# Four layer-norm affines of a two-block transformer step, moved from the passages between phases into the phase that follows

## The chip, the cores and the metric

One core of one Trainium2 chip runs the whole program. The metric is the device time of one execution in microseconds (us), taken over several runs; lower is better. Five engines work side by side, each through its own queue of instructions in a fixed order: PE (matrix multiply into PSUM), DVE (vector), ACT (activation), POOL (GpSimd) and SP, which issues most of the loads.

## The reference

One sequence of 512 tokens, 1024 features, all in float32. Two blocks stand one behind the other, and the program runs them as six phases: `mix` (hybrid mixer), `moe` (16 experts), `mla` (latent attention), `mlp0`, `s5` (a state-space mixer with a gated output) and `mlp1`. Every phase ends in the same step:

```python
x = layer_norm(ALPHA * x + gate * f(h), g, b)     # g, b: 1024 features
h = normalised(x) * (1 + scale) + shift           # what the next phase works on
```

The next phase needs two things of this: `h`, at once, as the input of its matrix products; and the new `x` itself, `normalised * g + b`, only when its own result is added onto it. For `mlp0` and `mlp1` the added row is `b + gate * b2`, b2 being the bias of the phase's second matrix.

## The kernel before

**Tiles.** X is one SBUF tile of [128, 4, 1024]: four token tiles of 128 tokens each. `h` is kept transposed (features on partitions) in two parts, `hh` and `hl`, whose sum is the float32 value, so that each product is three matmuls (`mm3`, lines 118 to 120). A part pair is made by `split_to` (lines 101 and 102): ACT writes the high part, DVE the low part as source minus high part.

**Rings.** Weights are loaded by SP into a ring of five buffers of 4 KB a partition (`wr`), split into rings of three (`wh`, `wl`), and multiplied. The fillers, generators that work out the modulation of later phases (`gemv`, lines 223 to 232), load through the same `wr` ring and add up on ACT, DVE (L228) and POOL (L232). The row tiles of a layer norm (`row_tile`) are taken from the `wr` ring too: g and b, each 512 KB as one row of 4 KB spread over all partitions, occupy two of its five buffers until they are used up.

**A passage.** A phase closes with `out_last` (or `combine` in `moe`): it loads its last weights, calls `begin_next`, and then runs the four token tiles through a pipeline. `begin_next` finishes the next phase's modulation, opens its `hh` and `hl`, and loads the two rows by `ln_rows` (with `b + gate * b2` for an mlp: two half rows of b2, two POOL multiplies at L371 and two POOL adds at L372). Each token tile is added up by DVE, gets its statistics (L296, L289, and the small column operations of `rsqrt`, L262 to L274, and L292), is normalised by ACT (L303), transposed by PE (L323), scaled and shifted out of PSUM by ACT (L333) and DVE (L331), and split into hh and hl. Then `affine_X` multiplies X[t] by g (L349) and adds b (L350), both on POOL, 128x1024 each. So a passage has eight POOL instructions of that size, and four passages have them: moe to mla, mla to mlp0, mlp0 to s5, s5 to mlp1.

**The places that the change names.** In `mla` the heads are walked in blocks of 128 queries, u = 0, 1, 2, ...; `probs` ends in the DVE scaling L468, kept as `self.scaled`. At u = 0 the weights of head 1 are loaded (`straight`, L529 and L530), at u = 4 those of head 2; at u = 5 the first three filler loads (L223) are given out, held by line 553 until the scaling of u = 4 is done; at u = 6 `rotated` loads the rotary weights of heads 2 and 3 (L514). In `mlp` the first three hidden features f = 0, 1, 2 are multiplied together, half of the tokens after the other (`mlp_first`), and each feature from f = 3 on loads its own 512 KB (L107). Their ReLU is L691, their square L692. In `s5` the gated output has eight features f, each with its own load of 512 KB and a tanh (L2159); after each of them one filler step follows.

**Order.** The tile framework puts each engine's instructions in order ahead of time, by program order and readiness. `after` makes an instruction wait for the end of another one; `hold` does so for what `self.behind` names (in the passage to `mla`, the last indirect gather onto X).

Of the kernel before, what the change touches and what calls it, by code (L numbers as in the profile page):

```python
# [15 lines left out]
D = 1024  # L16
T = 512
NT = 4
# [19 lines left out]
class Kern:  # L38
    def __init__(self, tc, io, ctx):
        self.tc, self.nc, self.io = tc, tc.nc, io  # L40
        nc = self.nc

        def pool(name, bufs, **kw):
            return ctx.enter_context(tc.tile_pool(name=name, bufs=bufs, **kw))

        self.cp = pool("const", 1)
        self.wrp = pool("wr", 5)
        self.whp = pool("wh", 3)
        self.wlp = pool("wl", 3)
        self.xp = pool("xres", 1)  # L50
        self.htp = pool("hT", 1)
        self.tmp = pool("tmp", 6)
        self.gap = pool("ga", 2)
        self.sm = pool("sm", 8)
        self.psA = pool("psA", 4, space=PSUM)
        self.psB = pool("psB", 4, space=PSUM)
        self.fillers = []
        self.behind = self.later = None
        self.consts()

    # ---------------------------------------------------------------- helpers
# [42 lines left out]
    def wload(self, src, kt, n):  # L104
        """src: [kt*128, n] view (or [128, kt, n]); gives the tile [128, kt, n] in two exact parts."""
# [10 lines left out]
    def mm3(self, out, lh, ll, rh, rl, st, sp):  # L116
# [3 lines left out]
        mm(out, ll, rh, start=False, stop=sp)  # L120
# [4 lines left out]
    def hold(self, load):  # L125
        """The load begins after what behind names, if anything."""
        self.after(load, self.behind)

    def after(self, inst, first):
        """inst begins when first, if anything, is done: what follows on first is urgent."""  # L130
# [4 lines left out]
    # ---------------------------------------------------------------- constants  # L135
    def consts(self):
# [11 lines left out]
        # mask[q, k] = 0 where k <= q, NEG elsewhere  # L148
# [6 lines left out]
    def vcols(self, name, parts):  # L155
        """Rows of 128 (features in order) put as columns: returns {key: [128, n] AP}."""
# [14 lines left out]
    # ---------------------------------------------------------------- modulation  # L171
# [15 lines left out]
    def gemv_cols(self, cond, w, n0, bcol, add, dst, p):  # L187
        """dst [128, 8] := part [n0, n0+1024) of cond @ w + b + add, feature-major; on both vector engines, and p
        [128, 8] in PSUM."""
# [23 lines left out]
    def gemv(self, ends, cond, w, b, n0, kind, dst, scale=1.0, bias=0.0):  # L213
        """Part [n0, n0+1024) of cond @ w + b. kind 'col': dst [128, 8] gets it feature-major;
        kind 'row': dst, a row of 1024 in DRAM, gets scale * it + bias. The sums over partitions of a half are put
        into ends and done some steps later, when what they need is there."""
# [40 lines left out]
    # ---------------------------------------------------------------- layer norm  # L257
    def rsqrt(self, out, v, n, eps):
        """out = (v + eps)^-0.5 for [128, n] columns: a guess from the exponent, three Newton steps."""
# [3 lines left out]
        # the guess is negative, and every step changes the sign  # L263
# [12 lines left out]
    def pipeline(self, gens, latest=True):  # L276
        """Generators of stages, each a stage behind the one before it; the latest or the earliest has the way."""
# [7 lines left out]
    def stats(self, st, eps):  # L285
        """From the bn_stats st of both halves: 1 / deviation and -mean / deviation."""
# [11 lines left out]
    def ln_tile(self, t, st, alpha, after):  # L298
        """Stages. X[t] normalised, st its bn_stats, then what follows on token tile t.
        (The norm of alpha times what X[t] holds, whose eps is alpha**2 times the one here.)"""  # L300
# [5 lines left out]
    def early(self, t, h, y, gate):  # L306
        """X[t] += gate * y for one half, y in PSUM (gate: what the reference multiplies by, over alpha)."""
# [6 lines left out]
    def to_hT(self, t, src, G, B, perm=False):  # L314
        """Stages. Token tile t (token-major src [128, 1024]) -> its columns of hT, times G plus B, in two parts.
        perm: token 256 h + 8 k + j stands at column 256 h + 32 j + k."""
# [29 lines left out]
    def affine_X(self, t, g, cb):  # L346
        """X[t] := X[t] * g + cb, off the main line."""
        nc = self.nc
        nc.gpsimd.tensor_mul(self.X[:, t], self.X[:, t], g)  # L349
        nc.gpsimd.tensor_add(self.X[:, t], self.X[:, t], cb)  # L350
# [8 lines left out]
    def ln_rows(self, g, b, gate=None, b2=None):  # L359
        """Row tiles g and b + gate * b2 on every partition."""  # L360
# [3 lines left out]
        self.bcast_row(gt, g, D)  # L364
        self.bcast_row(bt, b, D)
        if b2 is not None:
            for h in range(2):
                c = slice(512 * h, 512 * h + 512)
                tt = self.t()
                self.bcast_row(tt, b2[c], 512)  # L370
# [4 lines left out]
    def mod_gen(self, cond, w, b, g_col, b_col, key, out, alpha, dram):  # L375
        """shift, scale -> G, B columns; (1 + gate) / alpha -> a row in DRAM."""
# [24 lines left out]
    def gate_tile(self, mod, pool=None):  # L401
        """The gate row of a phase on every partition, loaded once."""
# [4 lines left out]
    # ---------------------------------------------------------------- rotary tables  # L407
    def rope_tables(self, pos):
        """A generator: cos and sin of the angles, token-major, and feature-major with the sign of the rotation."""
# [46 lines left out]
    # ---------------------------------------------------------------- softmax attention block  # L456
    def probs(self, S, n, scale=1.0):
        """Rows of exp(scale * (S - max)) / sum for a score block S [128, n] in PSUM, in SBUF."""
# [12 lines left out]
    # ---------------------------------------------------------------- latent attention  # L471
    def mla(self, q_norm, kv_norm, gate, after_tile):
# [37 lines left out]
        def rotated(hd):  # L510
            """The rotary halves of the queries of heads hd and hd + 1."""
# [30 lines left out]
        for u in range(4 * 8 + 2):  # L542
            hd, b = divmod(u, 4)
            if hd < 8:
# [6 lines left out]
                P[u] = self.probs(S, n, QK_SCALE)  # L551
                if u == 4:
                    self.later = self.scaled
# [27 lines left out]
    def mla_z(self, t, p, Z, q_norm, kv_norm):  # L581
        """Stages. Norms of the latents, rotation of the shared key; all feature-major in two parts."""
# [38 lines left out]
    def out_half(self, O, w, k0, gate):  # L621
        """Feature-major parts O (k-tiles k0..) times rows of w, token-major, onto X."""
# [14 lines left out]
    def out_last(self, O, w, k0, alpha, gate, after_tile, ring=0):  # L637
        """The same for the last parts, the gate taken into w, token tile by token tile and on through the layer norm.
        (ring: how many of w's pieces wait where other weights go.)"""
# [34 lines left out]
    # ---------------------------------------------------------------- squared-relu MLP  # L674
    def mlp(self, l, b1c, gate, after_tile):
# [4 lines left out]
        for c0, c1 in zip(cuts, cuts[1:]):  # L680
            A = []
            P = self.mlp_first(w1) if c0 == 0 else {}
            for f in range(c0, c1):
# [7 lines left out]
                nc.scalar.activation(a, p, AF.Relu, bias=b1c[:, f:f + 1])  # L691
# [10 lines left out]
    def mlp_first(self, w1):  # L702
        """The first hidden features; all of them on the first half of the tokens before the second one, whose
        layer norm may still be under way."""
# [8 lines left out]
    # ---------------------------------------------------------------- hybrid mixer  # L713
# [7 lines left out]
    def proj_in(self, col, n=128):  # L721
        """Feature-major columns [col, col + 128) of h @ w_in, in a PSUM bank."""
# [6 lines left out]
    def mix_load(self):  # L729
        """The input, normalised."""  # L730
# [17 lines left out]
    def mix_hT(self, X, G, B):  # L748
        """Feature-major h in two parts."""
# [30 lines left out]
    def mix_consts(self):  # L780
# [3 lines left out]
        # columns of dt (rows 0-31) and f (rows 32-47): sign, bias  # L784
# [8 lines left out]
        # -exp(a_log) on every partition  # L793
# [4 lines left out]
        # oh[r, h] = 1 where r % 32 = h  # L798
# [4 lines left out]
        # tri4[s, c, l] = 1 where s <= l  # L803
# [4 lines left out]
        # 1 / min(t + 1, w) over the first 16 tokens  # L808
# [31 lines left out]
    def dt_and_f(self, pool, dram):  # L840
        """dt, its decay sums over a chunk, and the forget sums; tokens on the partitions, but for the
        rows of heads acs (decay sums, in DRAM) and nF (forget sums, in two parts)."""
# [11 lines left out]
        # softplus(y) = max(y, 0) + log1p(exp(-|y|)); log1p(u) = 2 atanh(u / (2 + u))  # L854
# [31 lines left out]
        # -log f, summed over all tokens up to each  # L886
# [12 lines left out]
    def conv_silu(self, j, p, out):  # L899
        """Channel tile j of the convolved, gated xbc: PSUM bank p -> out."""  # L900
# [11 lines left out]
    def gate_th(self, b, k):  # L912
        """tanh(g / 2) of branch b's gate, feature tile k: sigmoid(g) = (1 + it) / 2."""
# [5 lines left out]
    def transpose4(self, src, n=NT):  # L919
        """The first n blocks of 128 columns of src, each transposed, in a PSUM bank."""  # L920
# [5 lines left out]
    def ssd(self, Y, dt, begun, between, behind):  # L926
        """The state-space mixer, through w_ssm_o, onto Y [128, 8, 512]. Its 16 pairs of heads go through
        the steps one behind the other; four pairs make a group, which shares B, C and the norm. The
        generator between adds work to the steps, the generator behind to the last ones."""
# [74 lines left out]
    def ssd_xt(self, i, r):  # L1004
        """x, token-major, times dt and times its decay to the chunk's end."""
# [12 lines left out]
    def ssd_states(self, i, q, r):  # L1018
        """The states that enter chunks 1 .. 3."""
# [15 lines left out]
    def ssd_scores(self, i, q, r):  # L1035
        """exp(min(sum(l) - sum(s), 0)) times C B, of both heads."""
# [11 lines left out]
    def ssd_y(self, i, q, r):  # L1048
# [11 lines left out]
        # the second head's products fill all partitions, then the first head's take the lower half  # L1060
# [29 lines left out]
    def ssd_norm(self, g, q):  # L1090
        """ys hold twice their values: a quarter of the squares, half the weights."""
# [44 lines left out]
    def attention(self, Y):  # L1136
        """A generator: forgetting attention; Y += (1 + tanh) * its output."""
# [22 lines left out]
        for u in range(len(units) + 2):  # L1160
# [12 lines left out]
            if 0 <= u - 1 < len(units):  # L1173
# [6 lines left out]
                else:  # L1180
                    # two blocks of queries go together
# [6 lines left out]
            if u >= 2:  # L1188
                pr, b, e = units[u - 2]
                # the second head's products fill all partitions, then the first head's take the lower half  # L1190
# [28 lines left out]
    def onto(self, Y, k, src):  # L1219
        """Y[:, k] (+)= src."""  # L1220
# [6 lines left out]
    def pool_branch(self, Y):  # L1227
        """A generator: averages over the last 2, 4, 8, 16 tokens, projected; Y += (1 + tanh) * that."""
# [68 lines left out]
    # ---------------------------------------------------------------- mixture of experts  # L1297
# [1084 lines left out]
```

## Time and profile before

| What | Value |
|---|---|
| Runs of the kernel before, us | 2886.74, 2892.04, 8444.8 |
| Median of the three, us | 2892.04 |
| Span of the profiled execution, us | 2884.3 |
| Mean granted TensorE clock | 0.930 |
| PE busy, share of the span | 2570.6 us, 89% |
| DVE busy | 1995.6 us, 69% |
| ACT busy | 1287.6 us, 45% |
| POOL busy | 779.2 us, 27% |

The profile is of one execution. It gives the span from the first to the last instruction, 2884.3 us; the two close runs are 2.4 and 7.7 us above that. A row of a timeline is: start in us, duration, engine, line, operation, out<-in, shape, count, and in brackets the engine's idle time before it and what ended that. In the table of stretches a row is: stretch, length, then busy time and count of PE, PEld (weight load), DVE, ACT and POOL, then the granted clock of TensorE (1.00 is 2.4 GHz, 0.50 is 1.2 GHz), the share of the DMA engines' time and GB/s.

### The profile page before, as it was taken

What the parts mean: (1) busy time and instruction counts of PE and PEld (TensorE: products, weight loads), DVE (VectorE), ACT (ScalarE), POOL (GpSimd) and SP (SyncE); (2) the same over time, 40 slices, a digit from 0 to 9 for tenths busy, and PEclk for the clock granted to TensorE, in tenths of its full rate; (3) what the DMA queues carried; (4) which work ended last, traced back from release to release, by engine and by line L of the source; (5) the groups of instructions that cost most, each with busy time, mean ns of one, the idle gap of its engine ahead of it and who ended that gap; (6) DMA issues with size and microseconds to landing.
All of it is one profiled execution on the core that took longest, in us unless ns stands there. A gap on an engine that the chain in (4) does not pass through costs nothing. (4 is left out here: it accounts for less than half of the span.)

```text
span 2884.3 us, 35607 instructions
## 1 busy us (share of the span) xinstructions
PE 2570.6 (89%) x12479; PEld 2085.8 (72%) x12479; DVE 1995.6 (69%) x3288; ACT 1287.6 (45%) x2125; POOL 779.2 (27%) x613
## 2 busy tenths in 40 slices
PE   6989899899999996798996898799999778899997
PEld 5778788687777775676774676677776577688885
DVE  7667577655666659779998776777667775943436
ACT  3445465534555421467774543453333534341422
POOL 2224333311112214221114123325334422500002
PEclk9989999899999896899997898899999889899998
DMA  7333244334444763789985343244554366333331
GB/s 220 86 90 103 74 120 124 98 89 139 140 136 149 224 214 117 240 284 328 373 296 127 103 132 88 79 120 123 137 140 146 126 197 187 113 107 95 97 101 59
DMA packets 378000, 427.03 MB, mean 148 GB/s; under 512 B 35415, under 2 KB 241162, under 8 KB 377818
## 3 DMA queue, kind: packets, MB, share of 16 engines
q1 hardware_dynamic: 371882, 404.26, 45.3%
q0 software_dynamic: 5936, 20.48, 2.3%
q8 instruction: 99, 1.62, 0.2%
q14 instruction: 83, 0.68, 0.1%
HBM read 390.19 MB, written 32.11 MB: 146 GB/s over the span
## 5 line engine op out<-in xcount | busy, mean ns | idle before, releaser
L102 DVE TENSOR_TENSOR wl<-wr,wh 128x1024 fp32r<-128x1024 f32 (+3 forms) x486 | 623.3, 1293 | 446.4 <-ACT wh L101 438.5
L101 ACT ACTIVATE wh<-wr 128x1024 fp32r<-128x1024 f32 (+3 forms) x486 | 493.4, 1027 | 670.0 <-PE pa L119 270.7
L118 PE MATMUL pa<-hh,wh 128*128 128x512 f32 (+1 forms) x1240 | 497.5, 401 | 7.5 <-ACT m L1237 5.2
L119 PE MATMUL pa<-hl,wh 128*128 128x512 f32 (+1 forms) x1240 | 488.9, 394 | 0.0
L120 PE MATMUL pa<-hh,wl 128*128 128x512 f32 (+1 forms) x1240 | 488.6, 394 | 0.0
L118 PEld LDWEIGHTS pa<-hh,wh 128*128 128x128 f32 (+1 forms) x1240 | 235.9, 190 | 61.4 <-ACT m L1237 5.8
L232 POOL TENSOR_TENSOR ga<-ga,wr 128x512 f32<-128x512 f32 x96 | 129.4, 1348 | 556.5 <-DVE ga L228 332.4
L120 PEld LDWEIGHTS pa<-hh,wl 128*128 128x128 f32 (+1 forms) x1240 | 235.3, 190 | 51.8 <-DVE wl L102 0.9
L119 PEld LDWEIGHTS pa<-hl,wh 128*128 128x128 f32 (+1 forms) x1240 | 236.0, 190 | 47.2 <-issue 0.7
L118 PE MATMUL pb<-wh,m 128*128 128x512 f32 x520 | 205.9, 400 | 12.6 <-DVE t L311 6.0
L118 PE MATMUL pb<-m 128*128 128x128 f32 (+8 forms) x616 | 194.6, 328 | 23.4 <-ACT m L101 22.8
L119 PE MATMUL pb<-wl,m 128*128 128x512 f32 x520 | 207.2, 398 | 2.2 <-DVE wl L102 2.2
L120 PE MATMUL pb<-wh,m 128*128 128x512 f32 x520 | 205.3, 397 | 0.0
L119 PE MATMUL pb<-m 128*128 128x128 f32 (+7 forms) x616 | 187.9, 313 | 3.0 <-DVE m L102 2.8
L120 PE MATMUL pb<-m 128*128 128x128 f32 (+6 forms) x616 | 185.0, 310 | 0.5 <-DVE m L102 0.5
L102 DVE TENSOR_TENSOR m<-t,m 128x512 fp32r<-128x512 f32 (+1 forms) x168 | 138.7, 831 | 59.0 <-ACT m L101 55.5
L101 ACT ACTIVATE m<-t 128x512 fp32r<-128x512 f32 (+1 forms) x168 | 101.6, 608 | 141.1 <-DVE t L692 90.6
L647 POOL TENSOR_TENSOR wr<-wr,gate 128x512 f32<-128x512 f32 x40 | 63.7, 1616 | 349.8 <-DMA wr<-in_mlp_w 297.2
L118 PEld LDWEIGHTS pb<-m 128*128 128x128 f32 (+2 forms) x616 | 115.1, 187 | 51.0 <-ACT m L101 25.3
L228 DVE SCALAR_TENSOR_TENSOR ga<-wr,cs,ga 128x512 f32<-128x512 f32 x128 | 101.3, 792 | 62.3 <-POOL ga L232 49.3
L230 ACT ACTIVATE wr<-wr,cs 128x512 f32<-128x512 f32 x96 | 69.4, 723 | 146.8 <-DMA wr<-in_mod_ffn_w 65.0
L119 PEld LDWEIGHTS pb<-m 128*128 128x128 f32 (+2 forms) x616 | 115.7, 188 | 17.2 <-DVE m L102 5.4
(709 smaller groups left out, 5479.2 us busy)
## 6 DMA issues: line engine op xcount, KB each, us to landing
wr<-in_mlp_w SPq DMA_DIRECT2D x128, 512.0 KB
wr<-in_w_in SPq DMA_DIRECT2D x96, 512.0 KB
wr<-in_w_exp_up SPq DMA_DIRECT2D x64, 512.0 KB
wr<-in_w_exp_gate SPq DMA_DIRECT2D x64, 512.0 KB
wr<-in_w_exp_down SPq DMA_DIRECT2D x64, 512.0 KB
wr<-in_w_ada SPq DMA_DIRECT2D x48, 512.0 KB
wr<-in_mod_mix_w SPq DMA_DIRECT2D x48, 512.0 KB
wr<-in_mod_ffn_w SPq DMA_DIRECT2D x48, 512.0 KB
```

The costliest lines, as they stand in the source:

```text
L101: self.after(self.nc.scalar.activation(hi, src, AF.Copy), first)
L102: self.nc.vector.tensor_sub(lo, src, hi.bitcast(F32))
L118: mm(out, lh, rh, start=st, stop=False)
L119: mm(out, lh, rl, start=False, stop=False)
L120: mm(out, ll, rh, start=False, stop=sp)
L228: nc.vector.scalar_tensor_tensor(acc, r[:, j], cond[:, k:k + 1], acc, op0=OP.mult, op1=OP.add)
L230: nc.scalar.activation(r[:, j] if k else acc, r[:, j], AF.Copy, scale=cond[:, k:k + 1])
L232: nc.gpsimd.tensor_add(acc, acc, r[:, j])
L647: self.nc.gpsimd.tensor_mul(r[:, j], r[:, j], gate[:, 512 * h:512 * h + 512])
```

## The change

`begin_next` no longer loads the rows at the four passages; it leaves a function, `self.owed`, that does. The next phase calls `settle` at one place: in `mla` behind the scaling of u = 3, in `mlp0` and `mlp1` behind the ReLU of f = 1, in `s5` behind the tanh of f = 0. There the rows are loaded, each load waiting for that instruction, and all four token tiles are multiplied and added on POOL, the eight instructions in a row. `affine_X` is gone. The rows' loads wait no longer for `self.behind`. The gate row of an mlp is now first asked for at the start of its phase, and not in `begin_next`. The passage mix to moe and the last norm stay as they were. The comments are left out of the changed file, and `mm3` returns its last instruction, which nothing uses.

```diff
-        self.behind = self.later = None
+        self.behind = self.later = self.owed = None
...
-    def affine_X(self, t, g, cb):
-        nc = self.nc
-        nc.gpsimd.tensor_mul(self.X[:, t], self.X[:, t], g)
-        nc.gpsimd.tensor_add(self.X[:, t], self.X[:, t], cb)
+    def settle(self, first):
+        rows, self.owed = self.owed, None
+        if rows is None:
+            return
+        gt, bt = rows(first)
+        for t in range(NT):
+            for op, row in ((self.nc.gpsimd.tensor_mul, gt), (self.nc.gpsimd.tensor_add, bt)):
+                self.after(op(self.X[:, t], self.X[:, t], row), first if row is gt else None)
...
-    def ln_rows(self, g, b, gate=None, b2=None):
+    def ln_rows(self, g, b, gate=None, b2=None, first=None):
         gt = self.row_tile()
         bt = self.row_tile()
-        self.bcast_row(gt, g, D)
-        self.bcast_row(bt, b, D)
+        row = lambda src, n: bass.AP(tensor=src.tensor, offset=src.offset, ap=[[0, 128], [1, n]])
+        self.after(nc.sync.dma_start(gt, row(g, D)), first)
+        self.after(nc.sync.dma_start(bt, row(b, D)), first)
         if b2 is not None:
             for h in range(2):
                 c = slice(512 * h, 512 * h + 512)
                 tt = self.t()
-                self.bcast_row(tt, b2[c], 512)
+                self.after(nc.sync.dma_start(tt, row(b2[c], 512)), first)
                 nc.gpsimd.tensor_mul(tt, tt, gate[:, c])
                 nc.gpsimd.tensor_add(bt[:, c], bt[:, c], tt)
...
                 P[u] = self.probs(S, n, QK_SCALE)
+                if u == 3:
+                    self.settle(self.scaled)
                 if u == 4:
                     self.later = self.scaled
...
-                nc.scalar.activation(a, p, AF.Relu, bias=b1c[:, f:f + 1])
+                relu = nc.scalar.activation(a, p, AF.Relu, bias=b1c[:, f:f + 1])
+                if f == 1:
+                    self.settle(relu.ins)
                 nc.vector.tensor_mul(a, a, a)
...
-            A.activation(a, p, AF.Tanh, bias=hb[:, f:f + 1], scale=0.5)
+            th = A.activation(a, p, AF.Tanh, bias=hb[:, f:f + 1], scale=0.5)
+            if f == 0:
+                self.settle(th.ins)
...
-                state["g"], state["b"] = K.ln_rows(io[g][l], io[b][l], K.gate_tile(mods[nxt]) if b2 is not None else None, b2)
+                rows = lambda first=None: K.ln_rows(io[g][l], io[b][l], K.gate_tile(mods[nxt]) if b2 is not None else None, b2, first)
+                if nxt and nxt != "moe":
+                    K.owed = rows
+                else:
+                    state["g"], state["b"] = rows()
...
                     yield from give(nxt, t, K.X[:, t])
-                    K.affine_X(t, state["g"], state["b"])
```

## Rows read from the trace of the kernel before

**Rows 1.** The page's part 1, busy time and share of the span.
```profile
PE 2570.6 (89%) x12479; PEld 2085.8 (72%) x12479; DVE 1995.6 (69%) x3288; ACT 1287.6 (45%) x2125; POOL 779.2 (27%) x613
```

**Rows 2.** Table of stretches: four passages, a restart, and places inside phases.
```profile
1540.00:1550.00 10.00, 0.00 (x0) 0.00 (x0) 5.22 (x33) 1.38 (x3) 0.00 (x0) 0.56 1.00 315
1554.00:1575.00 21.00, 10.93 (x39) 8.04 (x37) 18.30 (x12) 15.36 (x37) 20.39 (x8) 0.58 0.12 34
...
1630.00:1650.00 20.00, 15.91 (x66) 11.43 (x65) 17.25 (x32) 13.36 (x32) 9.62 (x7) 0.84 0.74 230
1801.00:1824.00 23.00, 5.08 (x24) 3.55 (x23) 22.46 (x59) 11.64 (x27) 14.55 (x6) 0.64 0.00 1
1840.00:1870.00 30.00, 30.00 (x148) 25.07 (x147) 24.76 (x58) 17.04 (x24) 5.44 (x7) 1.00 0.38 113
2242.00:2262.00 20.00, 4.22 (x14) 2.87 (x13) 19.83 (x24) 12.81 (x23) 15.41 (x7) 0.50 0.11 39
...
2495.00:2508.00 13.00, 4.55 (x19) 3.89 (x19) 12.90 (x12) 10.16 (x24) 13.00 (x8) 0.50 0.00 1
2508.00:2514.00 6.00, 5.94 (x28) 5.94 (x29) 6.00 (x8) 2.99 (x6) 6.00 (x3) 0.50 0.01 3
2530.00:2545.00 15.00, 15.00 (x68) 12.42 (x67) 8.16 (x10) 6.61 (x10) 0.00 (x0) 1.00 0.44 121
```

**Rows 3.** Groups by form, 2494 to 2522 us, the passage s5 to mlp1.
```profile
L102 DVE TENSOR_TENSOR hl<-t,hh 128x512 fp32r<-128x512 f32 x8 | 18.8, 2413 | 0.0
L350 POOL TENSOR_TENSOR X<-X,row 128x1024 f32<-128x1024 f32 x4 | 11.2, 2825 | 0.0
L349 POOL TENSOR_TENSOR X<-X,row 128x1024 f32<-128x1024 f32 x4 | 10.3, 2583 | 0.0
```

**Rows 4.** Groups by form, DVE, 2530 to 2610 us, mlp1 with POOL idle.
```profile
L102 DVE TENSOR_TENSOR wl<-wr,wh 128x1024 fp32r<-128x1024 f32 x15 | 18.4, 1225 | 35.7 <-ACT wh L101 35.7
L102 DVE TENSOR_TENSOR m<-t,m 128x512 fp32r<-128x512 f32 x13 | 9.0, 692 | 7.8 <-ACT m L101 7.7
```

**Rows 5.** DVE's timeline in the passage mla to mlp0: two column operations.
```profile
1803.82 2.26 DVE L270 SCALAR_TENSOR_TENSOR rt<-ri,ra 128x1 f32<-128x1 f32 x1
1806.11 2.26 DVE L274 SCALAR_TENSOR_TENSOR rs<-rt,ri 128x1 f32<-128x1 f32 x1
```

**Rows 6.** ACT's timeline, one row of each passage, in order of time.
```profile
1548.48 2.22 ACT L101 ACTIVATE m<-wr 128x448 fp32r<-128x448 f32 x4 [20.29 <-DMA wr<-in_mla_w_in]
...
1808.60 1.24 ACT L303 ACTIVATE X<-X,nb,rs 128x1024 f32<-128x1024 f32 x1 [7.33 <-DVE nb L292]
...
2252.11 1.24 ACT L303 ACTIVATE X<-X,nb,rs 128x1024 f32<-128x1024 f32 x1 [5.87 <-DVE nb L292]
...
2500.76 1.24 ACT L303 ACTIVATE X<-X,nb,rs 128x1024 f32<-128x1024 f32 x1 [1.88 <-DVE nb L292]
```

**Rows 7.** SP's timeline (SPq: issues), passage moe to mla and inside mla.
```profile
1538.59 0.36 SPq L123 DMA_DIRECT2D row<-in_ln_ffn_g  x1
...
1577.32 0.46 SPq L530 DMA_DIRECT2D wr<-in_mla_w_kvb  x1
1625.73 1.39 SPq L223 DMA_DIRECT2D wr<-in_mod_mix_w  x3
1627.23 0.92 SPq L514 DMA_DIRECT2D wr<-in_mla_w_qb  x2
```

**Rows 8.** Timelines of SP and POOL: one 512 KB row, issue to first use.
```profile
2490.82 0.34 SPq L123 DMA_DIRECT2D gate<-grow_mlp  x1
...
2494.70 2.49 POOL L371 TENSOR_TENSOR t<-t,gate 128x512 f32<-128x512 f32 x2 [16.75 <-DMA gate<-grow_mlp]
```

**Rows 9.** Timelines of ACT and PE in mlp1: ReLU of f = 1, first matmul of f = 3.
```profile
2527.36 0.67 ACT L691 ACTIVATE t<-pb,V 128x512 f32<-128x512 f32 x1
...
2529.20 0.40 PE L118 MATMUL pa<-hh,wh 128*128 128x512 f32 x1
```

**Rows 10.** The instructions of line 468, durations in ns: least, median, longest.
```profile
L468 DVE TENSOR_SCALAR t<-t,se x96: 254/400/1299, 685.2 to 1769.4; 128x128 f32<-128x128 f32 x24, 128x256 f32<-128x256 f32 x24, 128x384 f32<-128x384 f32 x24, 128x512 f32<-128x512 f32 x24
```

More of the change, by code (lines that the diff above doesn't have):

```diff
@@ L119, in mm3 @@
         mm(out, lh, rl, start=False, stop=False)
-        mm(out, ll, rh, start=False, stop=sp)
+        return mm(out, ll, rh, start=False, stop=sp)
     def bcast_row(self, dst, src, n):
```

## The prediction

> **What bounds the kernel now.** I read the page first: PE is busy 89% of the span, DVE 69%, POOL 27% [rows 1]. So the time is PE's work plus its holes, and a change of POOL's work counts only where it opens or closes a hole of PE. The table of stretches shows where they are: in the passages mla to mlp0, mlp0 to s5 and s5 to mlp1 PE is busy 5.1 of 23 us, 4.2 of 20 and 4.6 of 13, at a granted clock of 0.50 to 0.64, while DVE is full; inside mlp0 and mlp1 PE is full and the clock 1.00 [rows 2]. Then I asked what fills DVE there. In the last passage a low part hl takes 2413 ns on the mean [rows 3]; the same subtraction of the same size takes 692 ns where POOL is idle [rows 4]. Operations on one column take 2.26 us [rows 5], as long as a POOL multiply of 128x1024. So DVE stands still while POOL runs an instruction on X, gets one instruction in, and waits again. POOL's eight instructions of a passage, 2.58 and 2.83 us each [rows 3], make 21.6 us, in which DVE gets eight such instructions done.
>
> **What the change takes away: four passages.** In each the saving is what DVE's stall holds up, as far as ACT's own work allows.
> - mla to mlp0: three column operations stall by about 2.1 us each [rows 5], so ACT normalises token tile 2 only at 1808.60, after 7.33 us of idle time [rows 6]; 6 us of it go. Behind that ACT is the next limit; the later stalls of DVE, some 6 us, give 2.5. Together 8.5.
> - mlp0 to s5: ACT's idle time before tile 2 is 5.87 us [rows 6], and four hl lose about 1.4 us each behind it, of which I count 4. Together 10.
> - s5 to mlp1: the idle time is 1.88 [rows 6], and eight hl lose 1.7 us each [rows 3, 4], of which the four of the first half of the tokens hold up PE, less what ACT needs. I take 6.
> - moe to mla: two rows of 512 KB are issued at 1538.59 ahead of mla's first weights [rows 7], and ACT waits for those until 1548.48 [rows 6]; at 315 GB/s [rows 2] the rows cost 3.3 us. DVE is 18.3 of 21 us busy with 12 instructions, ACT 15.4 [rows 2]; with ACT as the limit 5.6 us of idle time go, and a little before and behind. I take 10.
>
> Sum 34.5. From below nothing (ACT or PE keeps the passage), from above PE's idle time in these stretches, 18 + 16 + 8 + 10 = 52.
>
> **What it adds: a wait in front of a ring.** The rows come out of the `wr` ring, and their loads wait for an instruction of the phase. What is the ring's rule for loads behind a waiting one? Inside mla the last free loads are issued by 1577.32, then three filler loads that must wait (line 553) at 1625.73, and right behind them at 1627.23 a load of weights that waits for nothing [rows 7]: 48 us in which it did not pass, although the ring's buffers were mostly empty. So I take it that a held load holds all later loads of its ring. Then:
> - mlp1: the load of f = 3 comes behind the rows. ReLU of f = 1 ends at 2528.03, and PE goes from f = 2 to f = 3 at 2529.20 [rows 9], without a gap now. Ahead of f = 3 lie two rows and two half rows, 1.57 MB, 5.0 us at 315 GB/s, then its own 512 KB, 1.7 us [rows 2]. One row of 512 KB takes 3.9 us from issue to use [rows 8], 2.2 more than its transfer. So f = 3 lands 8.9 us after the ReLU, ACT's split adds 1.1 (an estimate, from DVE's 1.2 for the same tile [rows 4]), and PE, which has 1.2 us of work left, stands still for 9. After such a stop the clock is 0.50 for 6 us of full work [rows 2], in the stretch from 2508 to 2514: 3 more. Sum 12.
> - mlp0: the same 12.
> - s5: behind the tanh of f = 0 there is no half feature left, and a filler load lies ahead of f = 1 in place of the half rows: 10.7, and 3 for the clock. Sum 13.7.
> - mla: the weights of head 2 and the rotary ones go behind the rows; with two buffers gone for POOL's 22 us, and fillers' buffers held until POOL adds them, the rotary load moves by some 10 us, and the scores of head 2 wait for it. I take 10 with the stalls of DVE there. From below 0, from above POOL's whole 21.6.
>
> **And the stall goes along.** POOL's eight instructions now stop DVE inside the phases. In mlp1 DVE is busy 8.2 of 15 us [rows 2] and has three blocked instructions a feature; PE has two features of split weights in hand: 2 us. In s5 four a feature: 3. In mlp0 DVE is busy 24.8 of 30 us beside a full PE [rows 2], much of it small fillers, each of which can wait 2.3 us [rows 5]; about 11 us of lag, part of which falls into PE's stop: 6. From below 0 each, from above 15 in mlp0, 8 in s5, 6 in mlp1.
>
> New costs: 10 + 18 + 16.7 + 14 = 58.7. Net 58.7 - 34.5 = +24 us on the profiled execution, 2884.3 to about 2908. The median of the runs lies 7.7 us above the span, so 2892.0 + 24 = 2916.
>
> A rule bears on the stall. DVE's scalings of the probabilities have a single SBUF input; their median is 400 ns, the longest 1299 [rows 10], so a POOL instruction stopped some of them. The Trainium skill (SBUF — State Buffer, Who interferes with whom) says that `tensor_scalar` in a 2-port mode and a DVE instruction with two SBUF inputs exclude a GpSimd instruction that reads SBUF, whoever issues first; the trace agrees. By it all the scalings in mla that fall into POOL's stretch wait, four of up to 2.7 us, which would make mla some 5 us dearer than I count, 2921 in all.
>
> **Rivals.**
> 1. *Faster: the later loads pass the held rows.* If the order in the queue can take f = 3 ahead of rows that are not ready, the stops of 9, 9 and 10.7 us and the clock's 9 go, and mla costs 5. Left are 5 + 6 + 3 + 2 = 16 against 34.5: 2892 - 18.5 = 2873.5. For it: SP is not in program order in everything (other pools' loads overtake). Against it: the 48 us in rows 7. It decides from one row on: the issue of f = 3 before or behind the rows.
> 2. *Faster still: POOL's work is hidden altogether there,* 2892 - 34.5 = 2857.5. Against it: DVE's 24.8 of 30 us in mlp0 and 17.3 of 20 in mla [rows 2]. The same skill page, Summary: rules for kernel authors, advises to put off whichever of the two engines is not on the critical path; by that rule this is the outcome.
> 3. *Slower: DVE's lag is not cushioned.* With the upper ends, 15 in mlp0, 8 in s5, 6 in mlp1, and 22 in mla, 30 us more: 2946. For it: mlp0's DVE has 5 us of slack in 30 [rows 2]. Against it: the stops give DVE time to catch up.
> 4. *Passages gain half,* since ACT and the matmuls at half clock keep them: +17, 2933. For it: ACT is 10.2 of 13 us busy in the last one [rows 2].
>
> **How the numbers follow.** Chances: forecast 0.56, first rival 0.18, second 0.04, third 0.13, fourth 0.09. The forecast alone has 2898 to 2934. The range 2870 to 2942 leaves out the second rival and most of the third: about 0.18. 2% of 2892 is 58 us, about what a measurement of this kernel can tell from no change: 2834 and 2950. Below lies nothing but a part of the second rival, 0.02; above half of the third and the tail of the forecast, 0.08; within 0.90.
>
> **What would show it.** Right: in the passages hl at 0.7 us and ACT's idle time before tile 2 near 1 us; in mlp0, mlp1 and s5 the rows' issues directly ahead of the load of f = 3 (f = 1 in s5), and a hole of PE of 8 to 11 us with a granted clock of 0.50 behind it; DVE instructions of 2 to 3 us inside mlp0. Wrong: a load of f = 3 ahead of the rows or a hole under 4 us (first rival); passages no shorter than now (fourth); holes of over 6 us in mlp0 behind the first one (third).

## The result, and the profile after

The changed kernel takes 2927.5 us (median of 2926.31, 2931.31, 2928.77 and 2922.49) against 2891.0 for the kernel before in the same sitting: a ratio of 1.013, interval 1.0106 to 1.0154 (the ratio leaves out one run of 8444.8 us). It is slower by 1.3%, less than the 2% that was called a difference, and the forecast said 2916 in 2870 to 2942. The profiled execution has a span of 2924.6 us, 40.3 more than before.

The page's part 1, against [rows 1], shows no engine with much more work: PE has the same 12479 matmuls, 16 us longer in all; POOL is busy 9 us longer, DVE 6 us shorter.

```profile
PE 2586.5 (88%) x12479; PEld 2098.8 (72%) x12479; DVE 1989.7 (68%) x3288; ACT 1288.0 (44%) x2125; POOL 788.4 (27%) x613
```

So the difference is where the work lies. Points that both traces have (starts, in us) give the sum, stretch by stretch:

| point | before | after | shift | of this stretch |
|---|---|---|---|---|
| end of the experts' last matmul | 1536.4 | 1547.2 | +10.8 | +10.8 |
| end of mla's first projections | 1593.7 | 1595.9 | +2.2 | -8.6 (passage) |
| norm of X, tile 0, end of mla | 1798.9 | 1812.9 | +14.0 | +11.8 (mla) |
| first ReLU of mlp0 | 1838.7 | 1843.9 | +5.2 | -8.8 (passage) |
| norm of X, tile 0, end of mlp0 | 2238.1 | 2266.3 | +28.2 | +23.0 (mlp0) |
| first tanh of s5 | 2393.9 | 2407.9 | +14.0 | -14.2 (passage and s5's front) |
| norm of X, tile 0, end of s5 | 2489.6 | 2525.1 | +35.5 | +21.5 (s5 behind the tanh) |
| first ReLU of mlp1 | 2524.5 | 2551.8 | +27.3 | -8.2 (passage) |
| ReLU of f = 7 in mlp1 | 2557.4 | 2598.5 | +41.1 | +13.8 (mlp1) |
| end | 2884.3 | 2924.6 | +40.3 | -0.8 |

The passages gave 39.8 back, the phases took 70.1. The first 10.8 lie ahead of anything changed: the order of all work up to there is the same in both. Fourteen profiles of this study, four with the scaling in its old place and ten with it put off, end that matmul anywhere from 1530.9 to 1549.4, so most of it belongs to the single execution, and below I compare only what lies behind it.

**The passages.** The table of stretches (columns as in [rows 2]): in the first tokens of the passages mla to mlp0, mlp0 to s5 and s5 to mlp1, PE is busy 18.0, 14.1 and 9.5 us where [rows 2] had 5.1, 4.2 and 4.6.

```profile
1815.00:1838.00 23.00, 18.00 (x109) 16.08 (x109) 16.60 (x74) 15.90 (x36) 0.00 (x0) 0.85 0.01 3
1847.00:1870.00 23.00, 5.94 (x31) 4.61 (x30) 20.93 (x33) 5.54 (x7) 13.53 (x7) 0.65 0.55 144
1870.00:1900.00 30.00, 30.00 (x123) 24.33 (x122) 24.68 (x25) 12.26 (x17) 17.86 (x12) 0.93 0.44 137
2270.00:2290.00 20.00, 14.09 (x64) 11.33 (x63) 14.93 (x34) 16.74 (x30) 1.29 (x1) 0.74 0.16 53
...
2530.50:2543.50 13.00, 9.45 (x45) 8.51 (x46) 7.81 (x16) 12.08 (x29) 0.00 (x0) 0.61 0.02 9
```

The group that showed DVE held up, the low parts in the passage s5 to mlp1, fell from 2413 ns [rows 3] to 688:

```profile
L102 DVE TENSOR_TENSOR hl<-t,hh 128x512 fp32r<-128x512 f32 x8 | 5.3, 688 | 3.2 <-ACT hh L101 3.2
```

**The phases.** The second row of the table above is the hole that replaces it, 1847 to 1870 in mlp0. SP's timeline there: the two rows (L370, L371) and the halves of b2 (L376) go out when the ReLU of f = 1 is done, and only behind them the weights (L107) of f = 3 to 5.

```profile
1847.44 0.35 SPq L370 DMA_DIRECT2D row<-in_ln_mix_g  x1
1847.84 0.43 SPq L371 DMA_DIRECT2D row<-in_ln_mix_b  x1
1848.37 0.85 SPq L376 DMA_DIRECT2D t<-in_mlp_b  x2
1849.27 6.60 SPq L107 DMA_DIRECT2D wr<-in_mlp_w  x3
```

PE's timeline, the first matmuls behind the releaser in mla, mlp0 (two rows), s5 (two rows) and mlp1. The bracket is PE's idle time; "wh" is ACT's part of weights that came late, "wl" DVE's.

```profile
1635.23 0.79 PE L118 MATMUL pa<-m,wh 128*128 128x512 f32 x1 [7.65 <-ACT wh L101]
...
1858.79 0.80 PE L118 MATMUL pa<-hh,wh 128*128 128x512 f32 x1 [8.93 <-ACT wh L101]
...
1868.15 0.79 PE L120 MATMUL pa<-hh,wl 128*128 128x512 f32 x1 [8.13 <-DVE wl L102]
...
2419.20 0.79 PE L118 MATMUL pa<-gh,wh 128*128 128x512 f32 x1 [11.35 <-ACT wh L101]
...
2423.15 0.79 PE L120 MATMUL pa<-gh,wl 128*128 128x512 f32 x1 [2.73 <-DVE wl L102]
...
2566.05 0.79 PE L118 MATMUL pa<-hh,wh 128*128 128x512 f32 x1 [8.53 <-ACT wh L101]
```

The hole of 8.13 us comes with POOL's burst (run 3, without the burst, has 0.15 in its place). DVE's timeline: filler operations of 128x32, 0.18 us each elsewhere, take 2.3 us beside POOL's burst on X (its row last). The high part of the weights is ready at 1857.68 + 1.06 = 1858.74 (ACT's row, which waited for the load behind the rows); DVE's low part gets its turn at 1866.88.

```profile
1851.22 0.18 DVE L1798 TENSOR_SCALAR rho<-rho 128x32 f32<-128x32 f32 x1
1851.43 2.31 DVE L1799 TENSOR_SCALAR ksc<-rho 128x32 f32<-128x32 f32 x1
1853.77 2.26 DVE L1800 TENSOR_SCALAR ksc<-ksc 128x32 f32<-128x32 f32 x1
...
1866.88 1.22 DVE L102 TENSOR_TENSOR wl<-wr,wh 128x1024 fp32r<-128x1024 f32 x1
```
```profile
1857.68 1.06 ACT L101 ACTIVATE wh<-wr 128x1024 fp32r<-128x1024 f32 x1 [5.93 <-DMA wr<-in_mlp_w]
```
```profile
1851.36 9.82 POOL L355 TENSOR_TENSOR X<-X,row 128x1024 f32<-128x1024 f32 x4 [83.93 <-DMA row<-in_ln_mix_g]
```

### The profile page after: what moved, and what is told of

The parts are those of the page before. It is cut to its first block, busy times and chain, and to the rows that moved or that the text cites. A ratio compares the mean times of both kernels' runs of the same rounds, so it can differ in the third digit from the quotient of the medians.

```text
span 2924.6 us, 35601 instructions
## 1 busy us (share of the span) xinstructions
PE 2586.5 (88%) x12479; PEld 2098.8 (72%) x12479; DVE 1989.7 (68%) x3288; ACT 1288.0 (44%) x2125; POOL 788.4 (27%) x613
## 3 DMA queue, kind: packets, MB, share of 16 engines
q1 hardware_dynamic: 371882, 404.26, 44.6%
## 5 line engine op out<-in xcount | busy, mean ns | idle before, releaser
L102 DVE TENSOR_TENSOR wl<-wr,wh 128x1024 fp32r<-128x1024 f32 (+3 forms) x486 | 634.7, 1316 | 458.8 <-ACT wh L101 448.8
L118 PE MATMUL pa<-hh,wh 128*128 128x512 f32 (+1 forms) x1240 | 504.1, 407 | 24.7 <-ACT wh L101 17.5
L120 PE MATMUL pa<-hh,wl 128*128 128x512 f32 (+1 forms) x1240 | 494.7, 399 | 8.7 <-DVE wl L102 8.7
L118 PE MATMUL pb<-wh,m 128*128 128x512 f32 x520 | 205.8, 400 | 15.3 <-DVE t L311 12.5
L118 PEld LDWEIGHTS pb<-m 128*128 128x128 f32 (+2 forms) x616 | 115.6, 188 | 56.7 <-ACT m L101 26.3
L355 POOL TENSOR_TENSOR X<-X,row 128x1024 f32<-128x1024 f32 x32 | 86.4, 2732 | 167.2 <-DMA row<-in_ln_mix_g 127.8
```

The lines of the kernel that those rows point to most:

```text
L102: self.nc.vector.tensor_sub(lo, src, hi.bitcast(F32))
L118: mm(out, lh, rh, start=st, stop=False)
L120: return mm(out, ll, rh, start=False, stop=sp)
L355: self.after(op(self.X[:, t], self.X[:, t], row), first if row is gt else None)
```

## The experiments

Theory H: the price is the held row loads, which keep the weights behind them from starting. Rival P: it is POOL's work on X, which holds up DVE in the phase as it did in the passage. Rival B: it is the two weight buffers that the rows take.

To compare profiles, each is cut at the norm of X's tile 0 (ACT, L303), so that a phase stands with the passage ahead of it; times in us, medians of the runs last. In the last column stands the ratio to the kernel before, timed in the same sitting.

| kernel | mla | mlp0 | s5 | mlp1 | behind the experts, with the tail | median | ratio |
|---|---|---|---|---|---|---|---|
| before (two profiles) | 262.5, 259.3 | 439.1, 437.4 | 251.6, 254.1 | 369.3, 370.6 | 1347.9, 1346.7 | 2887.5 to 2892.5 | |
| after (two profiles) | 265.7, 261.5 | 453.4, 455.1 | 258.8, 258.8 | 376.1, 377.0 | 1377.4, 1375.8 | 2927.5, 2920.9 | 1.013, 1.011 |
| rows_unheld | 264.3 | 453.6 | 256.4 | 368.4 | 1365.9 | 2902.9 | 1.0049 |
| rows_pool_queue | 267.5 | 453.1 | 264.2 | 364.9 | 1374.0 | 2918.4 | 1.0104 |
| after_no_scaling | 257.6 | 439.6 | 255.0 | 375.6 | 1351.1 | 2888.7 | 1.0016 |
| unheld_no_scaling | 245.1 | 431.3 | 245.0 | 361.5 | 1306.5 | 2853.0 | 0.9881 |
| before_no_scaling | 250.6 | 425.1 | 243.8 | 360.6 | 1305.5 | 2846.8 | 0.987 |
| spread_pool | 250.9 | 454.0 | 257.4 | 361.5 | 1349.0 | 2896.5 | 1.0025 |
| spread_dve | 245.5 | 436.2 | 253.2 | 364.2 | 1322.4 | 2865.5 | 0.9906 |
| spread_dve_gated | 253.0 | 443.7 | 246.1 | 361.8 | 1328.1 | 2868.1 | 0.9932 |
| before_dve | 249.7 | 431.7 | 249.4 | 369.4 | 1323.5 | 2873.8 | 0.9938 |
| mixed_dve | 251.7 | 432.2 | 247.6 | 363.6 | 1318.4 | 2864.7 | 0.9907 |

**1. The rows not held.**

```diff
-        gt, bt = rows(first)
+        gt, bt = rows()
```

> The changed kernel, but the row loads (and those of b2) wait for nothing; only POOL's first multiply still waits for the phase's instruction. Theory H (the held loads on SP keep the weights behind them from starting): the four stops of TensorE right behind the releasers, 7.7 in mla, 8.9 in mlp0, 11.4 in s5 and 8.5 in mlp1, sum 36.5 us, go; the smaller later ones, 8.1 in mlp0 and 2.7 in s5, stay, because POOL still slows VectorE. 2927.5 - 36.5 = 2891, within 2880 to 2905. Rival P (POOL's multiplies on X are what stops the phase, the hold is only beside them): not under 2915. Rival B (it is the two of five weight buffers that the rows take that starve TensorE): the rows now take them earlier, so 2925 or more.

2902.87 us, 1.0049 (1.003 to 1.0068): within H's range, near its upper end, and 12 us above its 2891. The four stops are gone: the rows are now issued well ahead of the releasers (mlp0's row of weight at 1767.72, the first ReLU of mlp0 starts at 1824.7), and no weight waits behind them. But mlp0 is not a bit shorter than in the changed kernel (453.6), and in s5 a new stop is longer than the old one. PE there waits for a filler's column sums, DVE for POOL's burst; timelines of PE, DVE and POOL:

```profile
2422.45 1.20 PE L244 MATMUL pa<-ones,ga 128*128 128x1 f32 x5 [18.25 <-DVE ga L240]
```
```profile
2400.71 5.66 DVE L2172 SCALAR_TENSOR_TENSOR t<-t,g 128x512 f32<-128x512 f32 x2
2406.29 2.83 DVE L2176 SCALAR_TENSOR_TENSOR zl<-t,zh 128x512 fp32r<-128x512 f32 x1
...
2419.49 2.82 DVE L240 TENSOR_TENSOR ga<-ga,t 1x512 f32<-1x512 f32 x1
```
```profile
2400.19 11.13 POOL L355 TENSOR_TENSOR X<-X,row 128x1024 f32<-128x1024 f32 x4 [2.34 <-ACT t L2169]
```

Each of these DVE operations lasts as long as one of POOL's, the addition on one partition (1x512) too. Rival B, by which the time had to be 2925 or more, falls.

**2. The rows held, but on POOL's queue.**

```diff
-        self.after(nc.sync.dma_start(gt, row(g, D)), first)
+        q = nc.sync if first is None else nc.gpsimd
+        self.after(q.dma_start(gt, row(g, D)), first)
```

(and so for the row of bias and b2.)

> The changed kernel, the row loads still released by the same instruction, but issued from POOL's queue in place of SP's: the two buffers are taken at the same place of the program and filled as late as in the changed kernel, and SP is free to issue the weights behind them. Theory H: about as the kernel with unheld rows, 2893 within 2880 to 2910, with no stop of 8 to 11 us right behind a releaser. Rival B (buffers): 2925 or more, the four stops stay. Rival P: not under 2915.

2918.36 us, 1.0104 (1.0083 to 1.0125): missed; not to be told from the changed kernel. Yet the profile does what H says of the stops. PE's first matmul behind the releaser waits 1.49 us in mlp0 (and 4.11 one feature on, for a low part), 3.77 in s5 and 1.78 in mlp1, so the weights passed the held rows. PE's timeline in mlp0 and s5:

```profile
1849.62 0.61 PE L118 MATMUL pa<-hh,wh 128*128 128x512 f32 x1 [1.49 <-ACT wh L101]
...
2417.19 0.79 PE L118 MATMUL pa<-gh,wh 128*128 128x512 f32 x1 [3.77 <-ACT wh L101]
...
2445.34 0.99 PE L244 MATMUL pa<-ones,ga 128*128 128x1 f32 x4 [13.03 <-DVE ga L240]
```

What held the loads back is therefore SP's queue, not the order in which the ring gives out buffers. In s5 a stop of 13.0 us waits for the same column sums as in run 1 (5.5 in the changed kernel). mlp1, where DVE has slack, gained 11 us, s5 lost 5. Why this kernel is 15 us slower than run 1, with the short stops of both, no run separates.

**3 and 4. Without the scaling, changed kernel and kernel before.** The eight POOL instructions on X are left out in both:

```diff
-        for t in range(NT):
-            for op, row in ((self.nc.gpsimd.tensor_mul, gt), (self.nc.gpsimd.tensor_add, bt)):
-                self.after(op(self.X[:, t], self.X[:, t], row), first if row is gt else None)
+        for row in (gt, bt):
+            self.nc.gpsimd.tensor_add(row[:, :1], row[:, :1], row[:, 1:2])
```

> The changed kernel without the eight multiplies and adds on X at each of the four passages (X times weight plus bias is left out; the row loads stay, held as before, and a small operation on one column reads each row). Theory H: the four stops of 36.5 us in all stay; what VectorE lost under POOL goes (8.1 in mlp0, 2.7 in s5, and the rest of the phases' growth, 11.8+23+21.4+13.8 = 70.0 less 36.5 less 10.9, in part): 2927.5 - 10.9 - 12 = about 2905, within 2890 to 2917. Rival P: the stops go as well, 2927.5 - 70 = 2858.

2888.74 us, 1.0016 (1.0003 to 1.0029): the stops stayed, as H says, but the time fell by 39, where H counted 23; it lies just under the lower end of H's range (2890) and far above rival P's 2858. PE's timeline: the stops in mlp0 and s5 are those of the changed kernel within 0.1 us, and DVE's low part comes 0.15 us late in place of 8.13.

```profile
1839.06 0.79 PE L118 MATMUL pa<-hh,wh 128*128 128x512 f32 x1 [8.96 <-ACT wh L101]
1840.43 0.79 PE L120 MATMUL pa<-hh,wl 128*128 128x512 f32 x1 [0.15 <-DVE wl L102]
```
```profile
2387.96 0.80 PE L118 MATMUL pa<-gh,wh 128*128 128x512 f32 x1 [11.44 <-ACT wh L101]
```

> The kernel before without the multiplies and adds on X at the four passages (X times weight plus bias is left out; the rows are loaded, a small operation on one column reads each). It prices the passages alone: the changed kernel's stretches from the end of one phase to the start of the next were shorter by 8.6, 8.8, 14.1 and 8.2, 39.7 us. Theory: the gain is all of POOL's work there, so 2891.0 - 39.7 = 2851, within 2843 to 2862. Rival (half of that gain was the row loads having left the front of SP's queue): 2871.

2846.79 us, 0.987 (0.9846 to 0.9894): as expected. The scaling costs the kernel before 40.7 us, and what leaves the passages is POOL's work, not the place of the rows' loads.

**5. Neither hold nor scaling** (both edits, 1 and 3).

> The changed kernel with both taken away: the row loads wait for nothing, and X times weight plus bias is left out (a small operation on one column reads each row). It is the fourth corner of a square whose other corners measured 2927.5 (held, scaled), 2902.9 (not held, scaled) and 2888.7 (held, not scaled). Theory O (hold and POOL's work overlap, each phase pays about the larger, so taking one away gives back less than it costs alone): 2850, within 2843 to 2860, as the kernel before without scaling (2846.8); then the hold alone costs 2888.7 - 2850 = 39 and the scaling alone 2902.9 - 2850 = 53, together 92 where both at once cost 77. Rival A (they add): 2902.9 + 2888.7 - 2927.5 = 2864. Rival B (rows in two of five buffers cost by themselves): 2870 or more.

2853.0 us, 0.9881 (0.9851 to 0.991): theory O, by which the two costs overlap. The square, by stretches behind the experts: nothing 1306.5, hold alone +44.6, scaling alone +59.4, both +70.9 and +69.3, where the sum would be 104. That is an overlap of 33 to 35 us, in single profiles. The ratios of the medians show less: 1.35% for the hold alone and 1.68% for the scaling alone, 3.03% in sum, against 2.49% and 2.29% for both, which is an overlap of 16 to 21 us, give or take some 13 by the intervals. So that the two overlap is shown, and by how much stays open.

By phase (hold, scaling, both): mla 12.5, 19.2, 20.6 or 16.4; mlp0 8.3, 22.3, 22.1 or 23.8; s5 10.0, 11.4, 13.8; mlp1 14.1, 6.9, 14.6 or 15.5. The kernel before without the scaling, which has neither cost, differs from this corner by 5.5 us in mla and 6.2 in mlp0, so a phase's figure is good to some 6 us. Within that each phase pays about the larger: in mlp0 POOL's burst, in mlp1 the hold. A likely reason, which no run tests by itself, is that DVE catches up with what POOL kept from it while PE stands for weights, and the other way round.

**6. The changed kernel, a second profile.**

> The changed kernel unaltered, a second profile. Its first one ended the last matmul of the experts 10.8 us later than the kernel before though the order of all work up to there is the same. Theory: that is a matter of the single execution, as this point lay between 1531.1 and 1547.2 in the six profiles so far; it ends anywhere from 1530 to 1548 here, and the stretches behind it add 29.5 (within 25 to 34) to those of the kernel before. Rival: the changed program makes it late, 1545 or more again. Ratio 1.013 in either case.

2920.9 us, 1.011 (1.008 to 1.014). The experts end at 1545.0, at the edge between the two, and the stretches behind add 27.9 to the first profile of the kernel before. The kernel before on VectorE and a second profile of the kernel before, both below, bear on it.

**7. POOL's work spread over four features.** A call per feature does one token tile, released by that feature's instruction; the rows are not held.

```diff
+        elif 0 <= t < NT and self.rows:
+            for op, row in zip((self.nc.gpsimd.tensor_mul, self.nc.gpsimd.tensor_add), self.rows):
+                inst = op(self.X[:, t], self.X[:, t], row)
+                self.after(inst, first if row is self.rows[0] else None)
```

> X times weight plus bias stays in the next phase and on POOL, but the rows are loaded without a wait, and the eight operations don't run in one burst: one token tile (a multiply and an add, 2.35 us each) is released by each of four features (mlp: f = 2 to 5, s5: f = 0 to 3 after its first load, here f = 1 to 4), and in mla by u = 5, 7, 9 and 11. Theory S (VectorE loses time only where a burst leaves it no slack; in mlp1 it is busy 36 of 75 us, in s5 27 of 48): mla, s5 and mlp1 hide it, mlp0 (VectorE busy 37 of 44 us) pays some 13; from 2850 that is about 2866, within 2855 to 2885. Rival: the 19 us of POOL's work cost the same wherever they lie: 2903, as with the burst.

2896.49 us, 1.0025 (1.0001 to 1.0048): theory S missed by 30. It holds in mlp1 (361.5, nothing paid) and nearly in mla (5.8 above no scaling), and fails in mlp0 (22.7) and in s5 (12.4), as dear as the burst. In s5 PE again stands 15.35 us for the column sums that come from DVE, in mlp0 8.56 for another DVE result (L311). So a mean slack of DVE does not hide POOL where PE waits for short links through DVE.

**8. The spread on VectorE.** As 7, with `vector` for `gpsimd` and no release.

> The same placing, rows not held, but VectorE does the multiplies and adds itself: eight operations of 128x1024, taken as 1.24 us each from VectorE's subtraction of that shape, 10 us a phase in place of 19 us in which POOL blocks it. Theory: hidden in mla, s5 and mlp1; in mlp0 VectorE goes from 37 to 47 of 44 us, some 4 us paid: 2855, within 2846 to 2872, faster than both kernels. Rival (what follows on VectorE, the weights' second part, is on the path in each of these phases): 10 us in all four, 2890.

2865.52 us, 0.9906 (0.9869 to 0.9943): within the theory's range, and faster than both kernels, than the kernel before by 0.9%. The groups of the 32 operations on X, POOL in the changed kernel and DVE here:

```profile
L355 POOL TENSOR_TENSOR X<-X,row 128x1024 f32<-128x1024 f32 x32 | 86.4, 2732 | 167.2 <-DMA row<-in_ln_mix_g 127.8 <-DMA row<-in_ln_ffn_g 39.3
```
```profile
L351 DVE TENSOR_TENSOR X<-X,row 128x1024 f32<-128x1024 f32 x32 | 38.1, 1218 | 17.0 <-PE pa L323 10.2 <-DMA row<-in_ln_ffn_g 4.4 <-POOL row L377 2.4
```

38.1 us of DVE stand for 86.4 of POOL in which DVE gets little done. But the operations did not lie where the program has them: those of the first passage ran from 1567.62 on, within it. So this run can't say whether putting them off helps at all.

**9 to 11. Is it the engine or the place?** `before_dve` is the kernel before with `vector` for `gpsimd` in `affine_X`, two lines; `spread_dve_gated` is run 8 with the release of run 7.

> The kernel before with its multiplies and adds on X at the four passages on VectorE in place of POOL, nothing put off. In the kernel with the spread on VectorE the eight operations took 1.22 us each, 9.8 us a passage, and many of them stood in the passages too. Theory (what the passages pay for is VectorE held up under POOL, 40.7 us by leaving the scaling out): VectorE is busy 18 of 30 us in such a passage, so most of the 9.8 fits beside the matmuls; 2846.8 + 4 x 4 = 2863, within 2853 to 2882, as good as the spread. Rival (VectorE is the bound of the passages, all 9.8 us are paid four times): 2886, no better than before.

2873.8 us, 0.9938 (0.9911 to 0.9965): within the theory's range, but almost half-way between its 2863 and the rival's 2886; above the kernel without scaling it is 6.8 us a passage, of the 9.8 that the operations take. The low parts in the passage s5 to mlp1 are undisturbed, with the operations on X beside them on the same engine:

```profile
L349 DVE TENSOR_TENSOR X<-X,row 128x1024 f32<-128x1024 f32 x4 | 5.7, 1434 | 5.8 <-PE pa L323 5.8
L102 DVE TENSOR_TENSOR hl<-t,hh 128x512 fp32r<-128x512 f32 x8 | 5.4, 683 | 0.2 <-ACT hh L101 0.2
```

> The spread on VectorE, where each token tile's multiply now waits for the ReLU, the tanh or the scaling of the probabilities of its feature or u. Without that wait the operations had run early, half of them still in the passages (1567.6 to 1580.6 and from 1801.6) and in s5 before the first tanh (2365.9 to 2377.4): those stretches were 5.9 and 7.2 us longer than with no scaling. Theory: these 13 us go and nothing comes in their place, 2865.5 - 13 = 2853, within 2846 to 2864. Rival (VectorE's queue waits with the gate, and the weights' second parts behind it): the mlp phases lose 3 to 6 us each, 2868 or more.

2868.14 us, 0.9932 (0.9911 to 0.9954), on the rival's side. s5 became 7 us shorter, as the theory says (246.1 from 253.2), but mlp0 grew from 436.2 to 443.7 and mla from 245.5 to 253.0.

> The kernel before unaltered, a second profile, for the point where the last matmul of the experts ends. Both profiles of the changed kernel have it at 1547.2 and 1545.0, the first of the kernel before at 1536.4, and kernels that share that order of work with the changed one at 1531.1 to 1548.9. Theory (a matter of the execution): anywhere from 1531 to 1549, and the rest of the span, 1347.9 in its first profile, is 1344 to 1352. Rival (the changed program is late there by itself): 1534 to 1538 again.

The experts end at 1540.8 and 1346.7 us lie behind, as the theory says. The kernel before on VectorE, with the scaling in its old place, has the experts' end at 1549.4, later than either profile of the changed kernel: a matter of the execution.

**12. Each passage in its shortest form.** Put off without a gate in mla, not put off at mla to mlp0, put off and gated in s5 and mlp1, all on VectorE.

> Each passage in the way that was shortest for it in the profiles, all on VectorE: from the experts to mla put off, not gated (245.5 us from the last expert matmul to the end of mla); from mla to mlp0 not put off (36.1 + 395.6 = 431.7 for the passage and mlp0, against 436.2 and 443.7 put off); to s5 and to mlp1 put off and gated (246.1 and 361.8). Theory (the stretches don't depend on one another): 245.5 + 431.7 + 246.1 + 361.8 + 23.3 = 1308.4 behind the experts, against 1347.9 and 1346.7 in the two profiles of the kernel before; a ratio of 2850/2891 = 0.986, 2850 within 2842 to 2860, faster than the spread (2865.5, 2868.1) and than VectorE alone (2873.8). Rival (the differences between these three are those of single executions): 1322 behind the experts and 2866.

2864.67 us, 0.9907 (0.9887 to 0.9926): the rival. 1318.4 us lie behind the experts, and mla alone came out 6.2 longer than in the profile from which it was picked. The four kernels on VectorE have intervals that overlap, so the place of the scaling, put off or not, makes no difference that these runs show; the engine makes 0.6 to 0.9%.

## Why the prediction was right, step by step

- *Passages.* Forecast 10, 8.5, 10 and 6, sum 34.5; measured 8.6, 8.8, 14.2 and 8.2, sum 39.8, and 40.7 by run 4. The rival that they gain half falls. The third was sized low: its figure takes in s5's front up to the first tanh. One sign came only in part: ACT's idle time before tile 2 in the passage mla to mlp0 fell from 7.33 to 4.19, not to near 1.
- *The wait in front of the ring.* Stops of 9, 9 and 10.7 us were worked out for mlp1, mlp0 and s5 (the terms that are written out give 10.0 for s5); they measured 8.53, 8.93 and 11.35, and stayed with no POOL work (9.07, 8.96, 11.44 in run 3). The clock behind them came as counted: 0.50 from 1868 to 1874 in mlp0, PE being busy 5.85 of the 6 us, and 0.50 from 2566 to 2572 in mlp1, busy 5.42. With the clock, 12, 13.7 and 12 were counted for mlp0, s5 and mlp1, and by the square the hold alone costs 8.3, 10.0 and 14.1. One word was wrong: "a held load holds all later loads of its ring". With the same ring and the hold on POOL's queue they passed (run 2); it is SP's queue that stands.
- *"And the stall goes along."* This is the step whose size failed, in mlp0 above all. It counted 6 us in mlp0, 3 in s5 and 2 in mlp1 on top of the hold. On top of the hold (both less hold alone in the square) POOL's burst added 13.8 to 15.5, 3.8 and 0.5 to 1.4; without the hold it costs 22.3, 11.4 and 6.9 (and 19.2 in mla), 59.8 over the four phases. In the first table the phases took 11.8, 23.0, 21.5 and 13.8 where 10, 18, 16.7 and 14 were counted, 70.1 against 58.7, and the passages gave back 39.8 for 34.5. The two errors, 11 and 5 us, have opposite signs in the sum. So it is in part luck that the total came out close, +24 forecast against +28 to +29.5 behind the experts and 32 to 37 by the medians.
- *First rival, 2873.5 if later loads pass.* Run 2 is its case: 2918.4. Run 1, with no load held, is 2902.9. Its 16 us for what is left was the same mis-sized term; the truth there is a kernel still slower than before.
- *Second rival, POOL's work hidden in the phases.* Only mlp1 hides it, mla nearly, and only spread out (run 7). The rule of the Trainium skill (SBUF — State Buffer, Summary: rules for kernel authors), "Schedule whichever is off the critical path", read as putting POOL's work off, doesn't pay here, as neither engine's work lies off the path in mla, mlp0 or s5: the burst alone costs more there (52.9 us) than the passages gave back.
- *Third rival, DVE's lag not cushioned.* Its sign did come: behind the first hole of mlp0 there are two of over 6 us, 8.13 and 6.26 (8.29 and 6.82 in the second profile), and mlp0 lost about the 15 us that the rival names. s5 and mlp1 did not lose its 8 and 6. What was said against it, that "the stops give DVE time to catch up", fits the overlap of the square, 16 to 35 us.
- *The rule on the stall.* The other rule of the Trainium skill (SBUF — State Buffer, Who interferes with whom), that a DVE instruction with two SBUF inputs and a POOL instruction that reads SBUF exclude each other, is what the rows of 2.82 and 2.83 us in run 1 show. Of the scalings in mla, which by the prediction's estimate would have cost 5 us more, none fell into the burst: POOL ran on X from 1631.49 to 1646.47 and from 1647.72 to 1652.45, while DVE waited for weights and split them. In run 1 two scalings fell into it: one took 2.23 us (128x256, elsewhere 0.35), the other 0.80 (128x384, elsewhere 0.41).

What was not tried: a hold on SP with POOL's work on DVE, fillers of mlp0 moved away from the burst, and second profiles of the square's other corners.

## What to carry to other kernels

A load that waits for an event costs what stands behind it in its issuing queue, so look what is behind it before you hold it. Here letting it go early gained 18 to 25 us; moving it to POOL's queue gained nothing that the runs can tell. Two costs in one phase need not add: find which wait ends last, and try each alone before adding them. Work on POOL that shuts out DVE is not hidden by a phase in which DVE has slack on the mean; the same operation on DVE, at 1.22 us in place of 2.73, was worth more than any of the places tried for it on POOL.

## What was not expected of the hardware

- Small DVE operations whose inputs lie in SBUF can wait out a POOL instruction whole: a filler's 128x32 with one input went from 0.18 us to 2.31, and an addition on one partition (1x512) took 2.82. Operations that read PSUM were not held: in mla two splits (ptl<-pa,pth), of 128x512 and of 128x128, took 0.88 us together at 1639.26, beside the burst. So in such a stretch the number of DVE's instructions with all inputs in SBUF says more than their size.
- Up to the end of the experts, with the same work in the same order, executions differ by 18.5 us (1530.9 to 1549.4), half of what the change is worth; in the stretch from 800 to 1000 us the granted clock was 0.92 in the profile of the kernel before and 0.86 in the first one of the changed kernel.
